# A hybrid decoder layer in float32: eight raw output weight rows requested in one go, diagonal term of the scan turned round, order of matmuls kept into the second half

## The chip, the core and the metric

The kernel runs on one core of a Trainium2 chip. The metric is the device time of one execution in microseconds (us), less is better. The core has five engines with instruction queues of their own: PE (TensorE, matrix products; its weight loads are listed apart as PEld), DVE (VectorE), ACT (ScalarE), POOL (GpSimd) and SP (SyncE, which here only issues DMA transfers). An engine works through its own queue in order; a semaphore holds an instruction until what it needs from another engine or from a transfer is there.

## The reference

One decoder layer for 1024 tokens of width 1024, with 16 meta tokens ahead, so L = 1040 positions, all in float32. The normalized input is projected to z, x, B, C, dt for a state space mixer (SSD, 16 heads of 64, two groups with a state of 128, chunks of 128 positions) and to q, k, v for a stick-breaking attention (16 heads of 64). Both results go through one output matrix, and a feed-forward part (width 2816, with a causal convolution over three positions) follows.

```python
xn = rms_norm(h, mix_pre_g)
proj = xn @ w_in                                  # z, xbc, dt_raw, q, k, v
# SSD, by chunks of 128 positions; the meta tokens are a chunk of 16
dt = softplus(dt_raw + dt_bias); A = -exp(a_log)
Acs = cumsum(dt * A)                              # within a chunk
Ldec = where(causal, exp(Acs[l] - Acs[s]), 0)
CB = einsum('bclgn,bcsgn->bgcls', Cc, Bc)
y_diag = einsum('bgcls,bgjcls,bcsgjp->bclgjp', CB, Ldec, Xdt)
states = einsum('bclgn,bgjcl,bclgjp->bcgjpn', Bc, exp(Acs[-1] - Acs), Xdt)
prev   = scan over chunks: carry * exp(Acs[-1]) + states
y_off = einsum('bclgn,bcgjpn,bgjcl->bclgjp', Cc, prev, exp(Acs))
y = (y_diag + y_off + xs * d_skip) * silu(z);  y_ssd = rms_norm(y, norm_g)
# stick-breaking attention
w[t,s] = beta[t,s] * prod over s<j<t of (1 - beta[t,j]),  beta = sigmoid(q.k / 8)
y_sb = rms_norm(w @ v, sb_norm_g)
mix = concat([y_ssd, y_sb]) @ w_out
h = h + rms_norm(mix, mix_post_g)
xn = rms_norm(h, ffn_pre_g);  gu = xn @ w_up
f = (gelu(causal_dwconv3(gu[:DFF])) * gu[DFF:]) @ w_down
h = h + rms_norm(f, ffn_post_g)
```

## The kernel before

**Precision.** A float32 operand of a projection is kept as two parts of a faster type, a rounded high part and the rest as a low part. A product then is three matmuls: high by high, high by low, low by high. `load_w` (L145) requests a raw weight block of 128 columns into a buffer `wraw` (two of them), ACT copies it into `whi` and POOL subtracts to get `wlo` (three buffers each). `project_steps` (L155) is a generator that yields after each of three stretches of positions (348, 346, 346 columns), eight blocks of the contraction by three matmuls each. `run(steps, n)` advances a generator by n yields, and `flow` strings several together. The source thereby interleaves work by hand: while one stage works through its chunks, `run(fill, ...)` puts projections for the next stage between them.

**Who sets the order.** Over most of the kernel a scheduler orders each engine's instructions by its own estimate. `tc.manual_schedule` (the ExitStacks `pe_order` and `order`) keeps the order of the source instead: for the PE during attention (`pe_order`, opened ahead of the loop over head pairs, closed at the end of it), and for PE, DVE, ACT and POOL from the sixth tile of the second output product on (`order`, opened at `t == 6`).

**Input (0 to 40 us).** For each of nine token blocks the input is normalized and transposed in two halves of four blocks (L215 to L222) into a PSUM tile of the pool `tp` (two tiles); ACT copies the high part `xh` from it, DVE subtracts the low part `xl`.

**First projections (40 to 190 us).** dt (16 columns), B and C of group 0 run side by side (`head`). dt is transposed to positions (`tpd`), DVE works through a chain of some twenty small instructions (softplus as a series), and `decays()` (L427) makes the cumulated decays with three pairs of small matmuls `pz_ea`, `pz_de`, `pz_cd` and exponentials on ACT. It stands after two steps of the first x projection. `bc[0][1][0]()`, the transposition of B, follows two steps later.

**SSD scans (190 to 460 us).** `scan_steps(g)` walks over nine chunks (one of 16 rows, eight of 128). `chunk_weights` (L450) makes `em`, the decayed and masked C by B of eight heads, `xdt`, the inputs times dt, and `yo`, the skip term. `chunk_outputs` (L486) makes the state, the diagonal term `yd` (eight products, `em` as the weights and 64 columns of `xdt` streamed), which DVE adds to `yo`, and the off-diagonal term `yf`. `chunk_store` (L518) transposes `yo` in four blocks into `tp`, multiplies by the gate `zk` and writes the result to memory (`yd` in DRAM, one tile for each 128 positions).

**Attention (460 to 1023 us).** A loop over eight head pairs `p` and eight query blocks `i`. `block_weights` makes logits `z` on the PE, two sigmoids `kp` and `bt` on ACT, the running product on DVE and the weights `bt` on POOL; `block_turn` transposes these (`tw`) and ACT copies them to `th`; `block_mix` multiplies with v (`av`). Projections of the next pairs fill in through `fill` until `p == 6, i == 5`, where they end. `avc` (L651) is the last product of a pair, for the edges of the blocks.

**Output products.** The output matrix has 16 rows of blocks of 128 x 1024, eight for the SSD half and eight for the attention half. `wout_steps` (L701) prepares one row a step: it requests the raw row into `wraw`, ACT scales it by the norm's gain into `wh` (L717, hence `wohb<-worb` in the second half), DVE makes the rest `wl`, and `halo_mm` (L708) multiplies the raw row with the two positions `y0` ahead of the tokens (`halo_y` loads them, two matmuls a row). The first half's rows (`wora`) are prepared from `p == 6, i == 5` on, two steps a block. `split_y` (L743) requests a tile `yk` of 128 positions from DRAM, ACT copies the high part `yh` (L748), POOL subtracts the low part `yl` (L749). `out_steps` makes two halves of 512 columns a tile, each 24 matmuls `mo` (L759) into one accumulator; `ssd_half` runs them for the eight tiles of the first half and writes them to `mixd`. These steps, `first`, are advanced from `p == 7, i == 2` on; what is left when attention ends runs in `for _ in first:` with one row of the second half between any two.

**Second half (1023 to 1181 us).** When attention has ended its memory is closed (`apool.close()`), and the pools `outp` and `est` are opened in its place. `second` prepares the rows `worb`. Then a loop over `t` from 1 to 8 makes the second output product of each tile, adds `mixd`, normalizes (`after`, with the mean squares `ms_mo`), and `turn_x2` transposes the result (`x2tp`, L918) for the feed-forward part. From 1181 us on the feed-forward part runs; its first product is `g0a` (L1068).

The names that the profile shows for DMA queues are those of the issuing engine (SPq is SP's). `f32` records of the PE come in pairs: one float32 matmul shows as two records.

## Time and profile before

| | before |
|---|---|
| device time, median of 3 runs | 1834.47 us (1833.14 to 1835.4) |
| the profiled execution | 1832.72 us |
| its span in the trace | 1831.0 us |
| mean granted clock of the PE over the span | 0.989 |
| bytes moved by DMA | 173.96 MB, 95 GB/s on average |
| share of PE in the chain that ended last | 47% of the span |

The profile was taken of one execution, whose own time is 1.7 us more than its span. Busy time counts records of an engine; matmuls are pipelined, so a record can begin before the one ahead of it has ended, and the time from start to start is what a matmul costs in a row of equal ones.

Three views are shown below. In the busy times by stage, a row is a window (from and to in us from the span's start), its length, then the busy us and the number of records of PE, PEld, DVE, ACT and POOL, the granted clock, the mean busy share of the DMA engines and GB/s. In the list of waits, a row is the waiting instructions, what released them, the total in us, the number of waits and the longest one. In the timeline, a row is the start in us, the length, the engine, line and operation, out<-in, shapes, how many records are drawn together, and in brackets the idle time before it and what ended it.

The 40 slices of the page tell the same coarsely: the PE is busy for nine tenths or more except in the first two, in the last, and in those that begin at 869.7, 1052.8 and 1144.4 us. The first of these three lies where attention runs without projections, the other two in the second output product.

### The profile page before, as it was taken

The numbers are of one execution on the slowest core, as the hardware profiler recorded it, in microseconds if no ns is written. First come the engines' busy times: TensorE is split into PE (matmuls) and PEld (weight loads), VectorE is DVE, ScalarE is ACT, GpSimd is POOL, SyncE is SP. The second block draws the span as 40 slices with busy tenths as digits, with TensorE's granted clock in tenths as the row PEclk, the third lists the DMA queues.
The fourth block names the chain that finished last, engine by engine and source line by source line (L and its number), as shares of the span: only waits on it lengthen the run. The fifth ranks groups of instructions, "written<-read, shape, count | busy, mean of one in ns | idle before, by whom it ended". The sixth has DMA issues, their size and how long they took to land.

```text
span 1831.0 us, 27362 instructions
## 1 busy us (share of the span) xinstructions
PE 1758.9 (96%) x10957; PEld 1508.3 (82%) x10957; DVE 1060.3 (58%) x1142; ACT 829.0 (45%) x1371; POOL 858.5 (47%) x613
## 2 busy tenths in 40 slices
PE   6899999999999999999799989899999999999997
PEld 5899889889888888888478767788889998888886
DVE  5551783574534544544722256766666666667988
ACT  5333454443655655655654243443333333344444
POOL 3213563485644644643764132276777776600001
PEclk9999999999999999999899999999999999999999
DMA  4123242231011110110232455233233333196344
GB/s 155 47 70 119 75 125 96 71 103 54 24 36 36 32 39 28 32 36 11 82 106 70 139 175 181 81 104 92 87 103 111 104 103 99 52 316 230 95 120 160
DMA packets 91443, 173.96 MB, mean 95 GB/s; under 512 B 11722, under 2 KB 36714, under 8 KB 91316
## 3 DMA queue, kind: packets, MB, share of 16 engines
q1 hardware_dynamic: 91316, 172.21, 29.9%
q8 instruction: 86, 1.41, 0.3%
q14 instruction: 41, 0.34, 0.1%
HBM read 122.39 MB, written 49.79 MB: 94 GB/s over the span
## 4 chain that ended last, share of the span: by engine, by line
PE 47%; DVE 3%; ACT 2%; POOL 1%; issue 1%; DMA 1%; POOLq 0%; SPq 0%; ACTq 0%; DVEq 0%
PE dn L1445 11%; PE fX L1054 9%; PE mo L759 6%; PE fY L1054 6%; PE fA L1054 6%; PE tw L617 1%; PE av L631 1%; PE z L596 1%; PE pj_v L163 1%; PE pj_q L163 1%; PE halo L708 1%; PE pj_k L163 1%; DVE oxn L912 1%; DVE mb L903 1%; POOL yl L749 0%
## 5 line engine op out<-in xcount | busy, mean ns | idle before, releaser
L601 DVE TENSOR_TENSOR_SCAN kp<-kp,hold 128x272 f32<-128x272 f32 (+7 forms) x128 | 206.7, 1657 | 202.3 <-ACT kp L597 99.6
L603 POOL TENSOR_TENSOR bt<-bt,kp 128x256 f32<-128x256 f32 (+7 forms) x128 | 213.8, 1688 | 195.9 <-DVE kp L601 143.3
L997 POOL TENSOR_TENSOR wl<-wr,wh 128x1024 fp32r<-128x1024 f32 x44 | 110.7, 2524 | 40.7 <-ACT wh L996 40.7
L1445 PE MATMUL dn<-dl,dh 128*128 128x512 f32 x308 | 120.1, 390 | 0.1
L1445 PE MATMUL dn<-dh 128*128 128x512 f32 x308 | 120.1, 390 | 0.0
L1445 PE MATMUL dn<-dh,dl 128*128 128x512 f32 x308 | 120.0, 390 | 0.0
L1491 POOL TENSOR_TENSOR fms<-fms,nhalf 128x1 f32<-128x1 f32 x8 | 8.5, 1060 | 225.8 <-DMA ar<-fda 186.0
L597 ACT ACTIVATE kp<-z 128x288 f32<-128x288 f32 (+6 forms) x112 | 82.7, 738 | 60.4 <-PE z L596 37.3
L1374 ACT ACTIVATE dh<-ar 128x512 fp32r<-128x512 f32 x77 | 48.7, 632 | 111.2 <-PE dn L1445 88.9
L996 ACT ACTIVATE wh<-wr 128x1024 fp32r<-128x1024 f32 x44 | 46.6, 1060 | 114.9 <-PE fX L1054 68.3
L596 PE MATMUL z<-k,q 64*128 64x144 f32 (+6 forms) x448 | 88.0, 494 | 8.3 <-ACT bt L598 3.9
L1126 DVE SCALAR_TENSOR_TENSOR ga<-gr,pp,ga 128x1024 f32<-128x1024 f32 x44 | 71.4, 1622 | 34.7 <-ACT ga L1119 34.0
L619 ACT ACTIVATE th<-tw 128x1024 f32<-128x1024 f32 (+2 forms) x96 | 74.4, 811 | 33.2 <-PE tw L617 31.1
L598 ACT ACTIVATE bt<-z 128x288 f32<-128x288 f32 (+6 forms) x112 | 83.0, 741 | 0.0
L617 PE MATMUL tw<-ident,bt 128*128 128x128 f32 x576 | 78.3, 282 | 4.4 <-POOL bt L603 2.9
L631 PE MATMUL av<-th,v 128*64 128x128 f32 x1152 | 78.1, 281 | 0.0
L631 PEld LDWEIGHTS av<-th,v 128*64 128x64 f32 x1152 | 62.6, 138 | 18.1 <-issue 17.3
L1375 DVE TENSOR_TENSOR dl<-ar,dh 128x512 fp32r<-128x512 f32 x77 | 53.2, 691 | 41.9 <-ACT dh L1374 41.8
L617 PEld LDWEIGHTS tw<-ident,bt 128*128 128x128 f32 x576 | 62.9, 143 | 15.9 <-issue 10.6
L596 PEld LDWEIGHTS z<-k,q 64*128 64x128 f32 x448 | 37.8, 191 | 39.0 <-issue 15.8
L1445 PEld LDWEIGHTS dn<-dh 128*128 128x128 f32 x308 | 57.8, 188 | 12.3 <-ACT dh L1374 0.3
L1445 PEld LDWEIGHTS dn<-dl,dh 128*128 128x128 f32 x308 | 57.9, 188 | 12.2 <-DVE dl L1375 0.4
(542 smaller groups left out, 5797.1 us busy)
## 6 DMA issues: line engine op xcount, KB each, us to landing
wr<-in_w_up SPq DMA_DIRECT2D x44, 512.0 KB
fds<-ga SPq DMA_DIRECT2D x44, 256.0 KB
b<-in_w_down SPq DMA_DIRECT2D x44, 256.0 KB
ar<-fds SPq DMA_DIRECT2D x44, 256.0 KB
fda<-ga SPq DMA_DIRECT2D x33, 256.0 KB
ar<-fda SPq DMA_DIRECT2D x33, 256.0 KB
yk<-yd SPq DMA_DIRECT2D x16, 512.0 KB
zd<-zt SPq DMA_DIRECT2D x8, 520.0 KB
```

The source lines that it names most:

```text
L596: mm(z[:, j, :w], q[h, t0:t0 + P], k[h, a:a + w], start=True, stop=True)
L597: nc.scalar.activation(kp[:, :, a:a + w], z[:, :, :w], AF.Sigmoid, scale=-QSCALE)
L598: nc.scalar.activation(bt[:, :, a:a + w], z[:, :, :w], AF.Sigmoid, scale=QSCALE)
L601: nc.vector.tensor_tensor_scan(kp[:, j][:, ::-1], kp[:, j][:, ::-1], hold[:, L - n:L][:, ::-1], 0.0, op0=ALU.mult, op1=ALU.max)
L603: nc.gpsimd.tensor_tensor(bt[:, j, 0:m], bt[:, j, 0:m], kp[:, j, 1:m + 1], op=ALU.mult)
L617: nc.tensor.transpose(tw[:, j, b, :], bt[:, j, c0:c0 + P], ident)
L619: nc.scalar.activation(th[:, :, :nb, :], tw[:, :, :nb, :], AF.Copy)
L631: mm(av[halves[j], :], v[:, kb, halves[j]], th[:, j, b, :], start=kb == 0, stop=kb == i)
L759: mm(acc, u[:, k, :], v[:, cs], start=(k == 0 and j == 0), stop=(k == 7 and j == 2))
L997: nc.gpsimd.tensor_tensor(l, raw, h.bitcast(F32), op=ALU.subtract)
L1054: mm(acc[:, c, :nn], u[:, k, :], v[:, k, c0:c0 + nn], start=first and k == 0 and j == 0, stop=k == 3 and j == 2, skip_group_check=not first)
L1445: mm(banks[t], u[:, 0, c], v[:, 1, :], start=(p == 0 and i == 0), stop=(p == NPR - 1 and i == 2))
```

## The change

It has eight parts.

1. The transposes of the input rotate over three PSUM pools (`tp`, `z`, `sd`, six tiles) instead of two tiles of `tp`.
2. dt: the high and the low part of its 16 columns lie side by side in one weight of 32 columns, so each of the eight blocks has two matmuls (with `xh` and `xl`) instead of three. The 32 rows are added up while they are turned to positions: nine products with a matrix `fold` (two identities) take the place of nine transposes.
3. `decays()` stands after four steps of the first x projections and after the transposition of B instead of ahead of them.
4. The diagonal term moves from `chunk_outputs` to `chunk_store`: `xdt` (64 columns) is the weight and `em` (128 columns) is streamed, the result comes transposed and goes into alternating halves of the partitions of `tp`, and the four transposes of `yo` add onto it. The addition on DVE and the accumulator `yd` are gone.
5. First half of the output weights: at `p == 6, i == 4` all eight rows are requested, into `wraw`, `wlo` and `whi` buffers in turn. Four rows are prepared at `i == 5`, the rest at `i == 6`, `halo_store` follows, and the first step of `first` comes at `i == 7` instead of at `p == 7, i == 2`. At `p == 7` one step runs at odd `i` and at `i == 6`. `halo_mm` runs for two rows at a time.
6. Second half: `yh1` (`halo_y`) and all eight rows are requested in one go, into two `wraw` buffers (rows 0, 1, 5, 6) and three new ones `wr` (2, 3, 4, 7). Two rows are prepared between any two steps of `first`, and the second tile is split ahead of the loop over `t`.
7. `pe_order` stays open until `t == 6`, so that the PE keeps the order of the source up to there.
8. A scratch size for dynamic DMAs is given (`dynamic_dma_scratch_size=2048`).

```diff
@@ input
             for hf in range(2):
-                tp = psum_tp(f"xtp{i}_{hf}")
+                tp = (psum_tp, psum_z, psum_sd)[(2 * i + hf) % 3](f"xtp{i}_{hf}")
+                if (2 * i + hf) % 3:
+                    tp = tp.rearrange("p (a b) -> p a b", b=P)
@@ dt
-        head = [project_steps(load_w(w_dt, 16, "dt"), 16, xh, xl, CH, dt_evac, "dt")]
+        fold = sp.tile([32, 16], F32, name="fold", tag="fold")
+        nc.vector.tensor_tensor(fold, ident[:32, 0:16], ident[:32, 16:32], op=ALU.add)
+        def dt_steps():
...
+            nc.scalar.activation(hl[:, :, 0:16], raw, AF.Copy)
+            nc.gpsimd.tensor_tensor(hl[:, :, 16:32], raw, hl[:, :, 0:16].bitcast(F32), op=ALU.subtract)
+            for c0, n in CH:
+                acc = psum_mm(f"pj_dt_{c0}")
+                for k in range(KB):
+                    for j, src in enumerate((xh, xl)):
+                        mm(acc[:32, :n], hl[:, k, :], src[:, k, c0:c0 + n],
+                           start=(k == 0 and j == 0), stop=(k == KB - 1 and j == 1))
+                nc.vector.tensor_copy(dtT[:, c0:c0 + n], acc[:32, :n])
+                yield
+        head = [dt_steps()]
...
-            nc.tensor.transpose(tpd[:nr, i * 16:(i + 1) * 16], dtT[:, c0:c0 + nr], ident[:16, :16])
+            mm(tpd[:nr, i * 16:(i + 1) * 16], dtT[:, c0:c0 + nr], fold, start=True, stop=True)
...
-        run(fill, 2)
+        run(fill, 4)
+        bc[0][1][0]()
         decays()
         tmp.close()
-        run(fill, 2)
-        bc[0][1][0]()
         run(fill)
@@ chunk_outputs
-            yg = psum_sd(f"yd{nm}").rearrange("p (h d) -> p h d", d=64)
-            for h in range(8):
-                mm(yg[:nr, h, :], em[:nr, h, :nr], xdt[:nr, h, :], start=True, stop=True)
-            nc.vector.tensor_tensor(yo[:nr], yg[:nr], yo[:nr], op=ALU.add)
@@ chunk_store
             for b in range(4):
-                nc.tensor.transpose(tp[:, b, :nr], yo2[:nr, b * P:(b + 1) * P], ident[:nr, :nr])
+                for j in range(2):
+                    mm(tp[halves[j], b, :nr], xdt[:nr, 2 * b + j, :], em[:nr, 2 * b + j, :nr],
+                       start=b == 0, stop=False, skip_group_check=True)
+            for b in range(4):
+                mm(tp[:, b, :nr], yo2[:nr, b * P:(b + 1) * P], ident[:nr, :nr], start=False, stop=True,
+                   is_transpose=True, skip_group_check=True)
@@ output weights
+    def raw_w(half, k, tile_):
+        wr = tile_ if tile_ is not None else wp.tile([P, D], F32, tag="wraw", name=f"wor{half}{k}")
+        r0 = (8 * half + k) * P
+        nc.sync.dma_start(out=wr, in_=w_out[r0:r0 + P, :])
+        return wr
...
-            wr = wp.tile([P, D], F32, tag="wraw", name=f"wor{nm}{k}")
-            r0 = (8 * half + k) * P
-            nc.sync.dma_start(out=wr, in_=w_out[r0:r0 + P, :])
+            wr = raws_.pop(0) if raws_ else raw_w(half, k, None)
...
             if len(todo) > 1:
-                halo_mm(*todo.pop(0))
+                for arg in todo:
+                    halo_mm(*arg)
+                todo.clear()
             yield
-        halo_mm(*todo.pop(0))
@@ attention loop
-            run(first, int(p == 7 and i > 4))
+            if p == 6 and i == 4:
+                ahead = [raw_w(0, k, None if k % 3 == 0 and k < 6 else wp_f32(("wlo", "whi", "wlo")[k % 3], f"wora{k}"))
+                         for k in range(8)]
...
-            if p == 7 and i == 1:
+            if p == 6 and i == 6:
                 run(wsteps)
                 halo_store(w1pool, 0, halo)
+                ys1 = [split_y(wp, 0, 1, ("whi", "wlo", WB))]
                 first = ssd_half(wres, ys1)
-            elif p > 5:
-                run(wsteps, 2)
-            if p == 7 and i == 0:
-                ys1 = [split_y(wp, 0, 1, ("whi", "wlo", WB))]
-            run(first, int(p == 7 and i > 1))
+            elif p == 6 and i == 5:
+                run(wsteps, 4)
+            run(first, int(p == 7 and (i % 2 or i > 5) or p == 6 and i == 7))
@@ after attention
     run(meta_steps)
-    pe_order.close()
     apool.close()
...
-    second = wout_steps(op, 1, sb_g, wres2, halo_y(op, 1, sb_g), halo)
+    y0b = halo_y(op, 1, sb_g)
+    ahead = [raw_w(1, k, None if k % 5 < 2 else est.tile([P, D], F32, tag="wr", name=f"worb{k}", bufs=3)) for k in range(8)]
+    second = wout_steps(op, 1, sb_g, wres2, y0b, halo, ahead)
     run(second, 1)
     ys = [split_y(op, 1, 1, ("yh", "yl", 2))]
     for _ in first:
-        run(second, 1)
+        run(second, 2)
     run(second)
+    ys.append(split_y(op, 1, 2, ("yh", "yl", 2)))
@@ second output product
         if t == 6:
+            pe_order.close()
             order.enter_context(tc.manual_schedule(engines=ORDERED))
-        if t < NT - 1:
+        if 1 < t < NT - 1:
             ys.append(split_y(op, 1, t + 1, ("yh", "yl", 2)))
@@ kernel
-    nc = bacc.Bacc("TRN2", target_bir_lowering=False, num_devices=1)
+    nc = bacc.Bacc("TRN2", target_bir_lowering=False, num_devices=1, dynamic_dma_scratch_size=2048)
```

More of the change, by code (lines that the diff above doesn't have):

```diff
@@ L371, in tile_layer @@
         nc.scalar.activation(expa, alog, AF.Exp)
-        dtT = rp.tile([16, L + 3], F32, name="dtT", tag="rt", bufs=1)
-        def dt_evac(acc, c0, n):
-            nc.vector.tensor_copy(dtT[:, c0:c0 + n], acc[:16, :n])
-        head = [project_steps(load_w(w_dt, 16, "dt"), 16, xh, xl, CH, dt_evac, "dt")]
+        dtT = rp.tile([32, L + 3], F32, name="dtT", tag="rt", bufs=1)
+        fold = sp.tile([32, 16], F32, name="fold", tag="fold")
+        nc.vector.tensor_tensor(fold, ident[:32, 0:16], ident[:32, 16:32], op=ALU.add)
+        def dt_steps():
+            raw = wp.tile([P, KB, 16], F32, tag="wraw", name="wr_dt")
+            hl = wp.tile([P, KB, 32], F32R, tag="whi", name="wh_dt", bufs=WB)
+            nc.sync.dma_start(out=raw, in_=w_dt)
+            nc.scalar.activation(hl[:, :, 0:16], raw, AF.Copy)
[9 more added lines that the diff above has]
+        head = [dt_steps()]
         bc = bc_flow(0)
@@ L516, in chunk_outputs, with chunk_store @@
             return yo, zk, nprev
-        def chunk_store(g, c, yo, zk):
+        def chunk_store(g, c, em, xdt, yo, zk):
             nr = NM if c == 0 else P
@@ L548, in scan_steps @@
                 yield
-                chunk_store(g, c, yo, zk)
+                chunk_store(g, c, cur[0], cur[1], yo, zk)
                 cur = nxt
@@ L699, in attend_meta, with wp_f32, wout_steps @@
         nc.gpsimd.tensor_copy(sq[:, M0:NM], sqm[:, 0, :])
-    def wout_steps(pool, half, gain, res, y0, acc):
+    def raw_w(half, k, tile_):
[3 more added lines that the diff above has]
+        return wr
+    def wp_f32(tag, name):
+        return wp.tile([P, 8, P], F32R, tag=tag, name=name, bufs=WB).bitcast(F32).rearrange("p a b -> p (a b)")
+    def wout_steps(pool, half, gain, res, y0, acc, raws_):
         nm = "ab"[half]
@@ L807, in tile_layer @@
                 halo = psum_mm("halo0")
[L808 to L809 removed]
+                wsteps = wout_steps(w1pool, 0, ssd_g, wres, halo_y(w1pool, 0, ssd_g), halo, ahead)
+            if p == 6 and i == 6:
                 run(wsteps)
                 halo_store(w1pool, 0, halo)
+                ys1 = [split_y(wp, 0, 1, ("whi", "wlo", WB))]
                 first = ssd_half(wres, ys1)
[L813 to L817 removed]
+            elif p == 6 and i == 5:
+                run(wsteps, 4)
+            run(first, int(p == 7 and (i % 2 or i > 5) or p == 6 and i == 7))
             if p == 7 and 2 < i < 6:
@@ L858, in tile_layer @@
     for _ in first:
-        run(second, 1)
+        run(second, 2)
     run(second)
-    def wp_f32(tag, name):
-        return wp.tile([P, 8, P], F32R, tag=tag, name=name, bufs=WB).bitcast(F32).rearrange("p a b -> p (a b)")
+    ys.append(split_y(op, 1, 2, ("yh", "yl", 2)))
     yraw[0] = wp_raw
```

1 line of the change is left out of this document (removed).

## The prediction

> **What bounds the kernel now.** I read the head of the page first, then the busy times of the engines by stage, then the list of what the PE waited for.
>
> ```profile
> span 1831.0 us, 27362 instructions
> PE 1758.9 (96%) x10957; PEld 1508.3 (82%) x10957; DVE 1060.3 (58%) x1142; ACT 829.0 (45%) x1371; POOL 858.5 (47%) x613
> ```
>
> ```profile
> 0.00:40.00 40.00, 22.35 (x121) 18.25 (x122) 23.86 (x42) 22.87 (x40) 14.23 (x24) 1.00 0.53 176
> 40.00:190.00 150.00, 143.57 (x897) 136.38 (x895) 61.51 (x71) 48.77 (x93) 34.95 (x22) 0.98 0.25 75
> 190.00:345.00 155.00, 151.33 (x956) 139.81 (x956) 97.53 (x109) 71.99 (x136) 77.95 (x63) 1.00 0.33 100
> 345.00:460.00 115.00, 112.29 (x683) 97.98 (x682) 73.72 (x98) 55.60 (x130) 78.66 (x81) 0.97 0.25 72
> 460.00:862.00 402.00, 400.54 (x3051) 338.19 (x3051) 184.71 (x141) 228.60 (x379) 216.29 (x169) 1.00 0.10 29
> 862.00:1023.00 161.00, 147.00 (x950) 106.52 (x949) 65.00 (x50) 85.62 (x136) 82.88 (x55) 0.97 0.28 86
> 1023.00:1181.00 158.00, 143.11 (x693) 112.78 (x692) 92.82 (x111) 64.84 (x105) 43.55 (x31) 0.97 0.49 157
> 1181.00:1831.00 650.00, 638.66 (x3618) 558.38 (x3616) 461.17 (x524) 250.67 (x357) 310.01 (x169) 1.00 0.39 125
> ```
>
> The stages are: the normalized input; the first projections; the SSD scans of the two head groups (190 to 345, 345 to 460); attention filled with projections; attention without them; the second output product; the feed-forward part. The first number after the length is the PE. It is busy in all but 72 us. In the SSD stages (3.7 and 2.7 us idle) a matmul less is time less; in the stages of 862 to 1181 (14.0 and 14.9 us idle) the order and the loads decide; behind 1181 the change touches nothing.
>
> ```profile
> PE xtp L219 <- DVE ms_pre L188: 10.3, 1, 10.3
> PE xtp L219 <- DVE xl L222: 6.0, 4, 2.2
> PE pz_ea L431 <- DVE s L419: 4.9, 1, 4.9
> PE g0a L1068 <- ACT gr L1074: 4.5, 1, 4.5
> PE x2tp L918 <- DVE ms_mo L188: 3.9, 1, 3.9
> PE yf L511 <- DVE pv L504: 2.9, 2, 2.0
> PE x2tp L918 <- DVE oxn L912: 1.7, 1, 1.7
> ```
>
> **The change part by part.** *Diagonal term of the SSD.* Before, eight products per chunk (two records each) load 128 columns of weights to stream 64. They become the same products turned round, 64 columns of weights and 128 streamed into alternating halves of the output. Attention has exactly this form in av, so the price is on the trace:
>
> ```profile
> 269.06 1.89 PE L507 MATMUL yd<-xdt,em 128*128 128x64 f32 x16
> 270.79 1.08 PE L511 MATMUL yf<-pv,ct 128*128 128x512 f32 x2
> ...
> 713.15 1.75 PE L631 MATMUL av<-th,v 128*64 128x128 f32 x28
> 714.83 1.97 PE L617 MATMUL tw<-ident,bt 128*128 128x128 f32 x16
> ```
>
> From start to start yd takes 1.73 us for 16 records, 108 ns each; av takes 1.68 us for 28, 60 ns each. A chunk saves 16 x 48 ns = 0.77 us, and 16 full chunks save 12.3 us (the two 16-row chunks are not counted). The PE is the bound there, so I count all of it. The 18 additions that leave DVE, and the accumulator that they read, I price at nothing: other work hid them, and the yf wait of 2.9 us, which they may ease, stays outside the sum. Bounds: 0, if DVE takes over as the bound, and 12.3 + 2.9 = 15.2 with the waits for yf gone too.
>
> The turned products are followed by full-width transposes, so the array's tiling changes twice in each chunk. [...] The trace has that very change from av to tw at 714.83, and tw starts before the 1.75 us of the last av are over. [...]
>
> *dt projection.* High and low weights share one 32-column load, so each k has two products instead of three: 24 fewer.
>
> ```profile
> 43.77 0.32 PE L163 MATMUL pj_dt<-xh,wh_dt 128*16 128x346 f32 x1
> ...
> 47.35 0.32 PE L163 MATMUL pj_dt<-xh,wl_dt 128*16 128x346 f32 x1
> ```
>
> These are the first and the last of 24 matmuls, (47.35 - 43.77) / 23 = 156 ns apart, so 24 x 0.156 = 3.7 us go. The copies of 32 rows, the nine small products with the folding matrix in place of nine transposes, and the one addition that builds that matrix cost nothing that I can see; all lie beside other projections.
>
> *Six accumulators for the first transposes instead of two.* The four waits for xl, 6.0 us, are the upper bound, 0 the lower. DVE limits the gain: behind the first wait of 10.3 us, 29.7 us of the first 40 are left, and DVE's 23.86 us lie nearly all in them, so under 6 us can close. The changed order also puts seven tiles' transposes ahead of the first dt product. I take a third of the waits, 2.1 us.
>
> *The decays moved back two projection steps and one transposition.*
>
> ```profile
> 64.19 2.70 DVE L313 TENSOR_SCALAR bt<-craw_B,pp 128x1040 f32<-128x1040 f32 x1 [4.64 <-ACT craw_B L310]
> 85.27 0.31 DVE L419 SCALAR_TENSOR_TENSOR s<-dt,expa 128x144 f32<-128x144 f32 x1
> 85.63 0.23 PE L431 MATMUL pz_ea<-s,tri 16*16 16x16 f32 x2 [4.89 <-DVE s L419]
> 87.85 0.49 PE L163 MATMUL pj_X<-xh,wh_X 128*128 128x348 f32 x1
> 88.72 0.49 PE L163 MATMUL pj_X<-xh,wh_X 128*128 128x348 f32 x1
> ```
>
> The DVE chain starts with the conv of the last B block (64.19) and is ready 21 us later; its order on DVE stays. In the changed order the decays stand 17 projection matmuls (2.7 us) later plus five transposes that came afterwards, but the scheduler keeps only that distance. The 4.9 us wait shrinks by 2.4 to about 2.5 us. Bounds: 0 (the chain slides as well) and 4.9 plus the slow matmuls behind it, (88.72 - 87.85) / 3 = 290 ns against 156, some 20 of them: 2.7 us more. I take 2.4, because 2.5 us of wait remain and the stage of 345 to 460 shows a granted clock of 0.97 with no wait longer than 2.0.
>
> [...]
>
> *First half of the output weights.* Eight raw rows go into eight buffers, two raw and six of the hi and lo buffers, as projections release them; the halo products come as two groups of eight; the first output products start at block 7 of head pair 6 instead of block 2 of pair 7, and are spread thinner.
>
> ```profile
> 878.45 1.03 PE L708 MATMUL halo<-wora,y 128*2 128x512 f32 x4
> 894.60 1.52 PE L596 MATMUL z<-k,q 64*128 64x344 f32 x4 [3.53 <-ACT bt L598]
> 1033.88 1.14 ACT L717 ACTIVATE wohb<-worb,pp 128x1024 fp32r<-128x1024 f32 x1
> ```
>
> A weight row gives the PE 1.03 us, so four rows in one block put 4.1 us of cover where the PE stood 3.53 us. But ACT scales each row, 1.14 us, and in the changed order seven rows, the eight halo copies and a yh stand ahead of the last sigmoids of those blocks, for which the PE waits. Bounds: -7.0 (half of the stage's 14.0 us idle), +4.6 (four scalings earlier, all on the path). I take -2.0, nearer to the middle because both act on the same wait.
>
> *Second half and the kept order.* Until the sixth tile the PE now follows the source: product step, two halo rows, product step, and so on. Before, the scheduler mixed them as data came.
>
> ```profile
> 1021.96 0.65 PE L651 MATMUL avc<-thc,vc 128*64 128x256 f32 x4
> 1024.34 2.40 POOL L662 TENSOR_TENSOR sq<-sq,sqb 128x1024 f32<-128x1024 f32 x1 [20.59 <-ACT sqb L661]
> 1026.88 0.32 SPq L747 DMA_DIRECT2D yk<-yd  x1
> 1032.93 1.05 ACT L748 ACTIVATE yh<-yk 128x1024 fp32r<-128x1024 f32 x1
> 1034.11 2.47 POOL L749 TENSOR_TENSOR yl<-yk,yh 128x1024 fp32r<-128x1024 f32 x1 [7.37 <-ACT yh L748]
> ```
>
> ```profile
> 1037.89 4.38 DMA worb<-in_w_out
> 1119.87 5.70 PE mo L759 x24
> ```
>
> Let T be the end of avc (1022.6). Attention's memory is free at 1026.7, and a transfer into it left at once: T + 4.3. In the changed order SP issues there the halo's y, then rows 2, 3, 4, 5, 6, the first yk of the second half, row 7, and only then the yk of tile 7 of the first half. Row 7 reuses the buffer of row 2, so it waits for a halo product on the PE, and tile 7 waits behind it. On the PE: a step to T + 5.7; y lands and is scaled by about T + 8, a wait of 2.3; two halo rows and a step to 15.8; two halo rows to 17.9. Row 7 goes at about 17, yk 0.3 later, landing 4.4 later (21.7), yh to 22.8, yl to 25.3. The PE stands 4.9 us, does one matmul and stands 2.4. New waits: 9.6 us. Of the old 14.9 us, g0a (4.5) and oxn (1.7) lie behind tile 6 and stay; the other 8.7 I let go, since 16 regular steps of 5.7 us give the norms time. Net +0.9. Bounds: -8.7 and, with transfers one behind another, +19.
>
> *Sum.* -12.3 - 3.7 - 2.1 - 2.4 - 2.0 + 0.9 = -21.6 us. The profiled execution took 1832.7 us, 1.7 more than its span and 1.8 less than the median of 1834.5; the sum gives 1811.1 by its own time and 1812.9 by the median. I say **1812 us**.
>
> **The rivals.** *Both transitions are covered.* The first output products fill every gap and the second half's loads come in time: -7.0 and -8.7 instead of -2.0 and +0.9, 14.6 us lower, 1797 us. For it: 28.9 us idle in these stages. Against it: ACT's load ahead of the sigmoids and row 7 ahead of yk.
>
> *DVE takes over in the SSD stages.* Half of the 12.3 us comes back as waits: 1818 us. For it: the yf waits on DVE. Against it: DVE is busy 97.5 of 155 us and loses work.
>
> *The early request brings nothing.* Rows are there, but ACT's scalings delay the sigmoids: +4.6 instead of -2.0, 1819 us. For it: the wait of 3.53 ends on ACT, not on a load. Against it: these scalings were in that stage before.
>
> [...]
>
> *Slower: the loads behind the attention queue up.* If the eight transfers from row 2 to yk land one behind another at x us each, the new waits are 2.3 + (4.7 + 8x + 3.5 - 17.9) = 8x - 7.4 us. The rest of the sum is -22.5, and 8.7 of old waits go, so the change loses from x = 4.8 on; at 5.2 it is 1835.5 + 2 for the slow clock behind such a wait, about 1837 us. For it: a single row took 4.38. Against it: the second half's stage moved 157 GB/s on average, 3.3 us for 512 KB, with pauses in it.
>
> **How the numbers follow.** Forecast 0.55, covered transitions 0.18, DVE 0.09, ACT 0.07, emptied array 0.03, queued loads 0.08. The likeliest case has its own range of 1804 to 1820. From 1798 to 1826 the range holds the forecast, the three cases near 1819 and nearly half of the covered case. Within 0.2% (3.7 us, about what a measurement of this kernel can tell from no change) lies 0.03 of the queued loads' chance, slower 0.05; faster 0.92.
>
> **What would show it right or wrong.** The turned products 60 ns apart; dt with 48 matmuls; the wait before pz_ea at 2.5 us; the SSD stages shorter by 12 us together with no new PE wait on DVE; a PE wait of about 5 us for yh or yl at the seventh tile of the first half, with row 7 just ahead of it on SP; no wait for ms_mo. The forecast is wrong if the turned products stay at 108 ns, if the stage of 1023 to 1181 grows by over 10 us, or if the first stages keep their length.

## The result and the profile after

The changed kernel takes 1812.9 us (median of 4 runs, 1811.4 to 1813.8) against 1834.9 us of before in the same comparison: a ratio of 0.9879, 95% interval 0.9862 to 0.9896. The forecast was 1812 us, between 1798 and 1826. The profiled execution of after took 1813.8 us, with a span of 1812.1.

So the sum came out. To see whether its terms did, the same points of the work are marked in both traces: the first or the last record of a name, from the timeline of the PE, in us from the span's start. The two traces differ by 18.9 us where the medians differ by 22.0, because the profiled execution of before was faster than all runs of before in this comparison and that of after was its slowest.

| point | before | after | gained up to here | forecast |
|---|---|---|---|---|
| dt turned to positions (first tpd) | 66.6 | 61.1 | 5.5 | 5.8 |
| first state product (st) | 189.2 | 182.0 | 7.2 | 8.2 |
| first attention logits (z) | 440.6 | 419.3 | 21.3 | 20.5 |
| last v projection ends | 863.9 | 841.3 | 22.6 | 20.5 |
| attention ends (avc) | 1022.6, 3 product steps left | 985.4, 6 left | | |
| first product of the second half (mo with wohb) | 1045.1 | 1038.6 | 6.5 | |
| first feed-forward product (g0a) | 1155.4 | 1136.6 | 18.8 | 21.6 |
| end of the span | 1831.0 | 1812.1 | 18.9 | 21.6 |

The product g0a begins at 1155.4 us in before, ahead of the 1181 us from which the description of that kernel lets the feed-forward part run. All of the gain lies ahead of 440 us. Between 440 and 864 us nothing was changed, and the 1.3 us gained there are no more than scatter: from the first z to the last product of the v projection the fourteen traces of this case take 421.4 to 423.4 us. Behind 864 us 3.8 us are lost again. That size is uncertain too: in the six traces with all of the change behind 864 us (after, e1, e6, e7, e8, e11) the stretch from the start of that product to g0a takes 292.6 to 296.5 us, against 291.8 in before. The busy times of both kernels between the last v projection and g0a show where; columns as before (window, length, then busy us and records of PE, PEld, DVE, ACT, POOL, granted clock, DMA share, GB/s). First before, in three stretches: the rest of attention, up to the second half's first product, up to g0a.

```profile
863.90:1022.60 158.70, 144.70 (x937) 104.29 (x935) 64.74 (x49) 85.03 (x135) 82.88 (x55) 0.97 0.28 88
1022.60:1045.10 22.50, 20.74 (x104) 15.53 (x103) 8.39 (x8) 8.30 (x10) 4.87 (x2) 1.00 0.46 133
1045.10:1155.40 110.30, 103.40 (x463) 79.43 (x463) 66.17 (x81) 43.51 (x74) 32.35 (x24) 0.97 0.54 175
```

The same three stretches after:

```profile
841.30:985.40 144.10, 126.10 (x864) 91.29 (x862) 70.16 (x49) 81.32 (x130) 81.16 (x53) 0.96 0.19 62
985.40:1038.60 53.20, 43.05 (x195) 30.89 (x195) 12.98 (x15) 21.29 (x28) 12.12 (x6) 0.90 0.54 184
1038.60:1136.60 98.00, 95.92 (x441) 78.70 (x442) 55.78 (x74) 34.40 (x60) 28.96 (x23) 0.98 0.47 157
```

Three more product steps of 5.7 us (24 products, 5.70 us in before), 17.1 us, are left for the second stretch. Moved back, attention's stretch would be 161.2 us against 158.7 (2.5 lost), the second one 36.1 against 22.5 (13.6 lost), and the third gives 12.3 back. The PE is idle for 10.2 us in the second stretch and its clock falls to 0.90. The list of the PE's waits after names the places (waiting instruction, releaser, total in us, how many, the longest):

```profile
PE xtp L221 <- DVE xn L213: 6.3, 4, 4.3
PE mo L783 <- ACT yh L772: 6.8, 1, 6.8
PE z L612 <- ACT bt L614: 6.0, 3, 4.7
PE tt_B L331 <- DVE bn L327: 2.9, 1, 2.9
PE yt L540 <- DVE yo L526: 2.8, 4, 1.2
PE mo L783 <- POOL yl L773: 2.5, 2, 1.7
PE x2tp L942 <- DVE ms_mo L188: 1.3, 1, 1.3
PE pz_ea L447 <- DVE s L435: 1.0, 1, 1.0
```

The waits of xtp for xl (6.0 us) have become waits for xn (6.3). Gone are those of yf (2.9) and most of that for pz_ea (4.9 became 1.0) and of that for ms_mo (3.9 became 1.3). New are those of mo for yh (6.8), of z for bt (6.0 instead of 3.9), of tt_B for a copy on DVE (2.9) and of the transposes of the output (yt) for their addition (2.8).

One gain stands in no list of waits. `halo_mm` now runs for two rows at a time, and two rows take the PE no longer than one. Two rows before, then four rows after:

```profile
887.11 1.89 PE L708 MATMUL halo<-wora,y 128*2 128x512 f32 x8
```

```profile
863.93 1.90 PE L733 MATMUL halo<-wora,y 128*2 128x512 f32 x16
```

The halo products of all 16 rows keep the PE busy for 14.2 us in before and for 8.0 us in after. Of the 14.2 us 5.1 lay in the third stretch, where five rows were still to be prepared; after has none there. Every run below keeps the rows in pairs, so these 6.3 us are read from the traces and not tested by a run.

The turned products themselves, and the transposes that follow in the other width, from the timeline after:

```profile
260.79 1.09 PE L537 MATMUL yt<-em,xdt 128*64 128x128 f32 x16
261.82 0.44 PE L540 MATMUL yt<-ident,yo 128*128 128x128 f32 x2
```

16 records take 1.03 us, 64 ns each instead of 108. The transposes start 0.06 us before the last product's record ends, so no time shows between the two widths.

The wait at the seventh tile of the first half, from the timelines after of SP, ACT and PE (one fence for each engine):

```profile
1000.04 0.33 SPq L720 DMA_DIRECT2D worb<-in_w_out  x1
1000.42 0.42 SPq L771 DMA_DIRECT2D yk<-yd  x1
```

```profile
1005.75 1.06 ACT L772 ACTIVATE yh<-yk 128x1024 fp32r<-128x1024 f32 x1 [0.59 <-DMA yk<-yd]
```

```profile
1006.86 0.80 PE L783 MATMUL mo<-woha,yh 128*128 128x512 f32 x1 [6.84 <-ACT yh L772]
1009.33 0.79 PE L783 MATMUL mo<-woha,yl 128*128 128x512 f32 x1 [1.68 <-POOL yl L773]
1011.20 0.63 PE L783 MATMUL mo<-wola,yh 128*128 128x512 f32 x1
1011.63 0.63 PE L783 MATMUL mo<-woha,yh 128*128 128x512 f32 x1
```

Row 7 of the weights leaves at 1000.04, when the halo products of rows 2 and 3 have ended, and yk of tile 7 right behind it. The tile lands 5.3 us later, ACT copies its high part, and the PE has stood for 6.8 us; it does one matmul and stands again for the low part. Then its records are 430 ns apart instead of 230: the last row begins at 1011.63, 0.43 us behind the one above it.

### The profile page after: what moved, and what is told of

It is laid out like the page before. It is cut to its first block, busy times and chain, and to the rows that moved or that the text cites. A ratio compares the mean times of both kernels' runs of the same rounds, so it can differ in the third digit from the quotient of the medians.

```text
span 1812.1 us, 27307 instructions
## 1 busy us (share of the span) xinstructions
PE 1738.3 (96%) x10942; PEld 1492.6 (82%) x10942; DVE 1062.2 (59%) x1125; ACT 831.7 (46%) x1373; POOL 863.4 (48%) x613
## 5 line engine op out<-in xcount | busy, mean ns | idle before, releaser
L647 PEld LDWEIGHTS av<-th,v 128*64 128x64 f32 x1152 | 62.8, 138 | 18.9 <-issue 17.9
L1400 DVE TENSOR_TENSOR dl<-ar,dh 128x512 fp32r<-128x512 f32 x77 | 53.2, 691 | 41.9 <-ACT dh L1399 41.9
```

What stands on the lines that cost most here:

```text
L647: mm(av[halves[j], :], v[:, kb, halves[j]], th[:, j, b, :], start=kb == 0, stop=kb == i)
```

## The experiments

Every time is the median of four runs unless it says otherwise, with the ratio to the kernel before of the same comparison.

### Each part of the first 440 us undone by itself

**e1: the diagonal term as before.**

```diff
+            yg = psum_sd(f"yd{nm}").rearrange("p (h d) -> p h d", d=64)
+            for h in range(8):
+                mm(yg[:nr, h, :], em[:nr, h, :nr], xdt[:nr, h, :], start=True, stop=True)
+            nc.vector.tensor_tensor(yo[:nr], yg[:nr], yo[:nr], op=ALU.add)
...
-                for j in range(2):
-                    mm(tp[halves[j], b, :nr], xdt[:nr, 2 * b + j, :], em[:nr, 2 * b + j, :nr], ...)
...
+                nc.tensor.transpose(tp[:, b, :nr], yo2[:nr, b * P:(b + 1) * P], ident[:nr, :nr])
```

> The changed kernel with the diagonal term as before (em as weights, 64 columns streamed, addition on DVE). Theory, the records of the turned products are 60 instead of 108 ns apart and the PE is the bound in the scans: 12.3 us slower than the changed kernel, up to 15.2 with the yf waits back, so about 1826 us, all of it between 182 and 439 us of the span, and the four yt<-yo waits (2.8 us) go. Rival, DVE had taken over as the bound there: only about 6 us slower. [...]

1832.6 us (10 runs), 0.9975 [0.9965, 0.9984]: 19.7 us slower than the changed kernel by the medians, 17.6 by the two ratios. From the first st to the first z the traces show 255.1 us against 237.3, 17.8 more. Two rows of busy times of e1, and two of after, for the two scans:

```profile
181.10:338.00 156.90, 154.02 (x952) 141.74 (x951) 96.55 (x108) 71.67 (x135) 77.07 (x63) 0.98 0.33 99
338.00:436.20 98.20, 95.50 (x575) 83.33 (x571) 70.16 (x87) 47.42 (x114) 65.23 (x59) 0.97 0.25 75
```

```profile
182.00:328.60 146.60, 145.26 (x952) 130.95 (x952) 96.72 (x99) 71.74 (x135) 78.63 (x63) 1.00 0.35 106
328.60:419.30 90.70, 86.99 (x574) 73.01 (x571) 70.02 (x77) 47.99 (x113) 68.53 (x60) 1.00 0.27 79
```

The idle time of the PE is 5.6 us in e1 and 5.1 in after: the yf waits of 2.9 us are exchanged for the yt waits of 2.8. So the difference is in the records, 16 x (1.73 - 1.03) = 11.2 us by their spacing, and in the clock, about 0.02 x 157 + 0.03 x 98 = 6 us. That DVE takes over as the bound is refuted, and the 0.06 us above show no loss between the two widths that would eat the gain. The clock's share was in no expectation, and part of it belongs to e1 alone: from the first st to the first z before takes 251.4 us, and so does e11 below, which has the diagonal term as before too. Against the 237.3 us of after that is 14.1 us for the term; the other 3.7 of e1's 17.8 us come with its lower clock (0.97 over this stretch, 0.99 in before and in e11).

**e6, e7, e8** (one profiled execution each; read at points of the trace, which is finer than the whole time). In e6 the dt projection has 72 matmuls and nine transposes again, in e7 the input transposes have two accumulators, in e8 the decays stand after two steps. In e6 and e7 the edit is part 2 and part 1 of the change in reverse; that of e8 is

```diff
-        run(fill, 4)
-        bc[0][1][0]()
+        run(fill, 2)
         decays()
         tmp.close()
+        run(fill, 2)
+        bc[0][1][0]()
```

> The changed kernel with the dt projection of 72 matmuls and nine transposes. Theory, 24 matmuls of 156 ns: the start of pj_X comes 3.7 us later less the 1.4 us that the nine products with fold took longer than nine transposes (2.1 against 0.7 us), so 2.3 us later. Rival, the wait for the DVE chain takes up what is saved: pz_cd ends at the same time, 88.6 us, within 1 us.

> The changed kernel with two accumulators for the first transposes. Theory as forecast: the last B block of the head ends 2.1 us later (61.2 becomes 63.3), with waits of xtp on xl of about 6 us. Rival, the six accumulators only move the waits from xl to xn and the transposes ahead of the first dt product: within 1 us.

> The changed kernel with the decays after two steps of the first x projection. Theory: the wait before pz_ea is about 5 us again, the wait of 2.9 us before tt_B goes, and the first state product st begins 1 to 2.5 us later than at 182.0. Rival, the chain of DVE slides and both orders wait alike: st begins within 0.5 us of 182.0.

The first st comes 2.5 us later in e6, 2.0 in e7 and 1.1 in e8; that is 5.6 of the 7.2 us gained at st, and no run shows what makes the rest. In e6 the first pj_X comes 1.9 us later and pz_cd ends 2.9 later; it is the matmuls less the dearer turning, not the DVE chain. The rows of tpd after and before show the dearer turning:

```profile
61.12 2.09 PE L406 MATMUL tpd<-fold,dtT 32*16 32x16 f32 x18
```

```profile
66.57 0.68 PE L390 MATMUL tpd<-ident,dtT 16*16 16x16 f32 x9
```

Nine products with fold are 18 records and take 2.1 us, nine transposes took 0.7. In e7 tpd begins at 63.1 instead of 61.1, as forecast, but not for the reason forecast: its waits of xtp are 16.8 us in sum (10.6 and 6.2) and those of after 16.9 (10.6 and 6.3). What after does not have is a wait of 1.7 us of the first dt product for its weights, which POOL is still making; in after more transposes stand ahead of that product. In e8 the wait ahead of pz_ea is 4.4 us, that ahead of tt_B is gone, and tt_X waits 1.1 us, which it does not in after: the move of the decays took 4.5 us of wait away and put 2.9 back. Why tt_B waits, from DVE's timeline after:

```profile
81.58 2.66 DVE L318 SCALAR_TENSOR_TENSOR xsT<-craw_X,pp,xsT 128x1040 f32<-128x1040 f32 x2
84.16 0.27 DVE L327 COPY bn<-tt_B 16x128 f32<-16x128 f32 x1
```

The transposes of B now come ahead of the decays and need a PSUM tile that DVE has to copy; that copy stands behind the chain for dt and the convolution of x.

### The transition into the second half

**e2: the kept order ended where it was before, at the end of attention.**

```diff
     run(meta_steps)
+    pe_order.close()
     apool.close()
...
         if t == 6:
-            pe_order.close()
             order.enter_context(tc.manual_schedule(engines=ORDERED))
```

> The changed kernel with the PE's kept order ended at the end of attention, where it was before. Theory, as forecast: the kept order lets go of the ms_mo and oxn waits in the second half (3.9 and 1.7 us before), and its price is that the PE can't take other work while it waits for tile 7; so without it one of these waits comes back and the tile 7 wait shrinks, within 3 us of the changed kernel in sum. Rival, the kept order brings the gain of the second half: 5 us or more slower. Rival, the kept order is what costs the 8.5 us at tile 7: 5 us or more faster.

1811.5 us, 0.9868 [0.9854, 0.9883]: not told apart from the changed kernel. In its profile the wait for yh is 4.2 us instead of 6.8, since the halo products came ahead, one of them waits 1.8 us for its row, and g0a begins 4.2 us earlier. The wait for ms_mo does not come back; it is 1.0 us. The one for oxn is 1.7 us instead of 0.3, but it is 1.5 to 1.8 us in e1, e6, e7 and e8 as well, which keep the order. So the kept order neither brings the gain of the second half nor makes its loss.

**e3: row 7 requested behind tile 7.**

```diff
-    ahead = [... for k in range(8)]
+    ahead = [... for k in range(7)]
...
-    for _ in first:
+    for n, _ in enumerate(first):
+        if n == 0:
+            ahead.append(raw_w(1, 7, est.tile([P, D], F32, tag="wr", name="worb7", bufs=3)))
         run(second, 2)
```

> The changed kernel with the request for row 7 of the second half behind that of yk for tile 7; nothing else moves. Theory, yk stood on SP behind row 7, which waits for a halo product on the PE: yk is issued about 995 instead of 1000.4 us, the wait for yh falls from 6.8 to 2 or 3 us, the slow clock behind it (mo records 430 ns apart instead of 230) shrinks, 5 to 8 us faster, about 1806 us. Rival, the transfers share the DMA engines (394 GB/s from 992 to 999 us) and yk is late for that: the wait stays above 5 us and the time within 2 us.

1811.5 us, 0.9868 [0.9852, 0.9885]. The expected 5 to 8 us did not come. Its timelines of SP, ACT and PE:

```profile
994.04 0.93 SPq L771 DMA_DIRECT2D yk<-yd  x2
...
1002.09 1.06 ACT L772 ACTIVATE yh<-yk 128x1024 fp32r<-128x1024 f32 x1 [0.29 <-DMA yk<-yd]
...
1003.20 0.49 PE L783 MATMUL mo<-woha,yh 128*128 128x512 f32 x1 [3.34 <-ACT yh L772]
1006.75 0.79 PE L783 MATMUL mo<-woha,yl 128*128 128x512 f32 x1 [3.05 <-POOL yl L773]
```

The tile is requested at 994.5, 6 us earlier, and yet lands only at 1002: 7.5 us for 512 KB, with six requests of the same size just ahead of it. The wait behind SP's queue was real, but behind it stood the transfers themselves. Both readings hold a part; 6.4 us of waits are left of 8.5, and the clock falls as before (mo records 0.42 us apart behind the second one).

**e4: tile 7 requested ahead of the rows.**

```diff
-            if t < NT:
+            if t < NT and t != 6:
                 ys.append(split_y(wp, 0, t + 1, ("whi", "wlo", WB)))
...
     y0b = halo_y(op, 1, sb_g)
+    ys1.append(split_y(wp, 0, 7, ("whi", "wlo", WB)))
```

> The changed kernel with tile 7 of the first half requested ahead of rows 2 to 7, as the first 512 KB after attention. Theory: yh and yl of tile 7 are there before the PE needs them; the waits of 6.8 and 1.7 us and the slow clock behind them (about 2.3 us) go, the rows come one transfer (1.3 us at 394 GB/s) later and may cost that once: 9 to 11 us faster, about 1803 us. Rival, the wait only moves to the rows, since the same bytes must land before the second half begins: under 3 us faster, with halo or mo waits on worb of 5 us or more.

1803.2 us, 0.9825 [0.9809, 0.9840]: 9.8 us faster than the changed kernel by the medians, and 10.9 at g0a. No wait for tile 7 is left, and no wait for one of the rows stands in its list. The order of the requests, and not their number, was the price.

**e12: the second half and its order as before, with the changed first half.**

```diff
+    pe_order.close()
     apool.close()
...
-    ahead = [raw_w(1, k, ...) for k in range(8)]
-    second = wout_steps(op, 1, sb_g, wres2, y0b, halo, ahead)
+    second = wout_steps(op, 1, sb_g, wres2, halo_y(op, 1, sb_g), halo, [])
...
-        run(second, 2)
+        run(second, 1)
...
```

> The changed kernel with the second half's rows requested one by one as before, one row between two product steps, and the scheduler's own order there; the first half stays changed, so six product steps are left when attention ends. Theory: no row stands ahead of tile 7 on SP behind a wait for the PE, and the six steps cover the loads: the wait of 6.8 us is gone, 4 to 9 us faster than the changed kernel, unless the halo's y is late as in e5 (13.3 us). Rival, the request of all rows in one go is what keeps the second half fed: 3 us or more slower.

1801.7 us, 0.9832 [0.9802, 0.9861]: 11.2 us faster than the changed kernel by the medians, 8.6 by the two ratios, which count a run of 1810.9 us among its four. At tile 7 one wait of 2.0 us for yl is left. Its busy times in the three stretches:

```profile
842.00:986.20 144.20, 125.32 (x865) 90.84 (x863) 69.88 (x49) 81.14 (x130) 81.15 (x53) 0.96 0.19 62
986.20:1027.90 41.70, 39.75 (x196) 29.02 (x195) 12.51 (x12) 17.98 (x22) 9.61 (x4) 1.00 0.62 203
1027.90:1124.70 96.80, 94.16 (x443) 77.64 (x443) 61.02 (x77) 37.71 (x67) 33.62 (x24) 1.00 0.52 173
```

The third stretch is 13.5 us shorter than that of before with the same requests and without the kept order. In it the PE is idle for 2.6 us instead of 6.9, the five rows' halo products (5.1 us) are gone, and the clock is 1.00 instead of 0.97, about 3 us. Six product steps are left in the second stretch instead of three, the rows are prepared in their cover, and none is left for the third. The run e5 below shows that this is not the only way to it. The request in one go and the kept order then only cost: the second stretch has 11.5 us more with them (53.2 against 41.7).

**e5: the first half as before, with the changed second half.**

```diff
-            if p == 6 and i == 4:
-                ahead = [raw_w(0, k, ...) for k in range(8)]
+            run(first, int(p == 7 and i > 4))
...
-                wsteps = wout_steps(w1pool, 0, ssd_g, wres, halo_y(w1pool, 0, ssd_g), halo, ahead)
-            if p == 6 and i == 6:
+                wsteps = wout_steps(w1pool, 0, ssd_g, wres, halo_y(w1pool, 0, ssd_g), halo, [])
+            if p == 7 and i == 1:
                 run(wsteps)
...
-            run(first, int(p == 7 and (i % 2 or i > 5) or p == 6 and i == 7))
+            run(first, int(p == 7 and i > 1))
```

> The changed kernel with the first half of the output weights as before (rows requested one by one, two prepared a block, first product step at block 2 of pair 7). Theory: the early request brought about nothing by itself, since the scalings, halo copies and yh on ACT ahead of the sigmoids cost a wait of 4.7 us and a slow clock behind it; time within 4 us of the changed kernel. Rival, as forecast: 2 us or more slower. Rival, the early rows are a loss: 3 us or more faster.

1814.9 us, 0.9894 [0.9877, 0.9910], within 4 us as expected, but not for the reason given. Its busy times in the three stretches, and a new wait in its list, which spoils the run as a measure of the scalings:

```profile
841.60:1001.70 160.10, 144.98 (x936) 104.51 (x934) 66.66 (x49) 85.38 (x135) 83.28 (x55) 0.96 0.26 87
1001.70:1039.90 38.20, 24.90 (x125) 16.75 (x123) 15.76 (x13) 15.52 (x19) 8.05 (x3) 0.82 0.51 167
1039.90:1137.30 97.40, 94.39 (x443) 77.50 (x443) 56.88 (x76) 35.91 (x64) 30.05 (x23) 1.00 0.48 163
```

```profile
PE halo L733 <- DVE y L753: 13.3, 1, 13.3
```

SP requests the halo's y only at 1014.56, after 5.0 us in which it waits for a transfer of mixd to end. The run answers another question, though. Its first half is as before and three product steps are left, and yet its third stretch is as short as that of e12 (97.4 and 96.8 us against 110.3): with two rows between any two steps all eight are prepared ahead of it here too. Either half of the change alone takes the third stretch down by about 13 us, and both together take it down once (12.3).

### What is left, and a version that beats both

**e9: e4, with the scalings of the first half spread and the halo's y loaded early.**

```diff
-            if p == 6 and i == 6:
+            if p == 6 and i == 7:
                 run(wsteps)
                 halo_store(w1pool, 0, halo)
-                ys1 = [split_y(wp, 0, 1, ("whi", "wlo", WB))]
                 first = ssd_half(wres, ys1)
+            elif p == 6 and i == 6:
+                run(wsteps, 2)
+                ys1 = [split_y(wp, 0, 1, ("whi", "wlo", WB))]
...
-            run(first, int(p == 7 and (i % 2 or i > 5) or p == 6 and i == 7))
+            run(first, int(p == 7 and (i % 2 or i > 5 or i == 0)))
...
-    y0b = halo_y(op, 1, sb_g)
+    ys1.append(split_y(wp, 0, 7, ("whi", "wlo", WB)))
+    y0b = halo_y(w1pool, 1, sb_g)
```

> The changed kernel with tile 7 requested first, the halo's y loaded into memory that is free before attention ends, and the first half's scalings spread: four rows at block 5 of pair 6, two at block 6, two and the halo copies at block 7, product steps from block 0 of pair 7 on. Theory: beside the 10 us of e4 the wait of z for bt (4.7 us) with the slow clock behind it (13 us at 0.76, 3 us) goes, and the 1.2 us ahead of the first halo product: 5 to 8 us faster than e4, about 1796 us. Rival, the scalings delay whatever sigmoids they stand among: the waits only move to blocks 6 and 7, within 2 us of e4.

1798.3 us, 0.9801 [0.9783, 0.9820]: 36 us faster than before by the ratio, and 4.8 faster than e4 by the medians (4.4 by the two ratios), a little under the 5 to 8 expected. What it removes is this queue on ACT in the changed kernel, ahead of the sigmoids that the PE waits for:

```profile
865.74 2.23 ACT L740 ACTIVATE woha<-wora,pp 128x1024 fp32r<-128x1024 f32 x2
867.82 1.56 ACT L761 ACTIVATE mh<-halo 2x256 f32<-2x256 f32 x4
869.39 1.06 ACT L772 ACTIVATE yh<-yk 128x1024 fp32r<-128x1024 f32 x1
870.48 0.75 ACT L613 ACTIVATE kp<-z 128x696 f32<-128x696 f32 x1
```

Two scalings, four halo copies and a yh take 4.7 us, as long as z waits. In e9 the longest wait for bt is 2.1 us, and attention's stretch takes 141.1 us instead of 144.2 in e4. Part of the wait moved, part is gone.

**e10: e9 with the edit of e2.**

> The kernel of e9 with the PE's kept order ended at the end of attention. Theory: the kept order cost 2 to 4 us only because the PE could not take the halo products ahead while tile 7 was late; without that stall it is worth nothing either way, within 2 us of e9. Rival, the scheduler's own order is better throughout: 3 us or more faster than e9. Rival, the kept order gains once the stall is gone: 3 us or more slower.

1799.9 us, 0.9811 [0.9792, 0.9830]: within 2 us of e9 as expected, and the two intervals overlap, though all four runs are slower than all four of e9. In the traces e10 has lost 2.4 us on e9 by the first z, far ahead of its edit, and from the end of attention to g0a both take 138.7 us. No worth of the kept order is seen either way.

**e11: only the parts from the output weights on; parts 1 to 4 of the change in reverse.**

> The changed kernel with the input transposes, the dt projection, the decays and the diagonal term as before, so that only the parts from the output weights on are changed. Theory: all the gain lies ahead of 460 us, and what comes behind is a loss of about 3 us by the two profiles: 0 to 5 us slower than before. Rival, as forecast: 1 us faster than before. Rival, the early rows and the kept order carry part of the gain: 5 us or more faster than before.

1836.5 us (10 runs), 1.0015 [1.0002, 1.0028], 2.7 us slower than before by the ratio. That agrees with the 3.8 us lost behind 864 us in the trace of after. Its own trace, of the fastest of its ten runs, loses 0.8 us there.

## Why the prediction was right

The total, the sign and the place of the gain were right, the sizes of several terms were not.

- **Diagonal term, -12.3.** Right in mechanism, close in size: 64 ns instead of 60 make 11.2 us, and with the clock and the waits before and after differ by 14.1 us between st and z, inside the bounds of 0 and 15.2. The additions, which the prediction priced "at nothing", hid an exchange: the yf waits went, as it allowed, and the remaining addition now stands straight ahead of the transposes for 2.8 us.
- **dt, -3.7.** The step that failed is that the nine small products "cost nothing that I can see": they take 1.4 us more than the nine transposes. Measured 2.5 at st.
- **Accumulators, -2.1.** Measured 2.0 in e7, but by luck. The forecast was a third of the waits for xl, and none of the waiting went: it moved from xl to xn (6.0 and 6.3 us). Of the 2.0 us 1.7 are the wait of the first dt product for POOL.
- **Decays, -2.4.** Measured 1.1. The wait ahead of pz_ea fell to 1.0, further than forecast. The step failed because it looked at the moved matmuls alone: the transposes of B, put ahead of them, wait 2.9 us for DVE. That its queue holds their copy behind the chain could be read from "its order on DVE stays".
- **First half, -2.0.** This step failed. By place, attention's stretch lost 2.5 us with the three steps moved back, and is 1.1 us longer than in e5, which has the first half as before. The cover was priced at 4.1 us for four rows; they take 1.90. And the longest wait of z for bt grew from 3.5 to 4.7 us, behind the queue on ACT that the prediction had named; its bound of +4.6 holds the result.
- **Second half with kept order, +0.9.** By place the second stretch lost 13.6 us and the third gave 12.3 back, +1.3, close in sum by other sizes. The new waits at tile 7 were told in place and order, 9.6 us, and measured 9.7 (6.8, 1.7, and 1.2 ahead of the first halo product). Their slow clock, 2.5 us (the 23 records behind the second wait take 8.0 us instead of 5.5), was counted only in the rival of the queued loads. Of the old waits 8.7 us were let go; in the third stretch 4.8 us of idle time went, and with it the five rows' halo products, 5.1 us, which no term holds. The prediction adds up its two terms for the halves. The runs do not: e12 and e5 each get the short third stretch from one half alone, so the second change brings it no second time. Behind the changed first half, the second half as before is 11.2 us faster by the medians.
- **Both halves together.** Their sum, -1.1, was about 4 us too good (2.7 are lost by e11 and 3.8 by the trace of after), although the halo products save 6.3 us that were not counted. That the total still came out at 1812.9 is in part luck: the first 440 us gave 0.8 more than forecast, and the medians happen to lie 3.1 us further apart than the two traces.
- **The rivals.** "Both transitions are covered" was not what the change does; e9 at 1798 us comes close to its 1797, with the requests put in another order. "Queued loads" is not settled by e3: one tile lands after 7.5 us there instead of 4.4, but the x of that rival is the distance from one landing to the next, about 1.3 us for 512 KB at the 394 GB/s from 992 to 999 us. Its sum at x = 5.2 comes to 3.0 us more than before, which is 1837.5 by the median and not 1835.5. For the emptied array of the chances (0.03) the trace of after shows no time: the transposes begin 0.06 us before the last turned product's record ends.

Not settled: how much of the scalings' 4.7 us could be had in a better place, what the pairs of halo rows are worth by themselves, and what the first half would do beside an unchanged second half and unchanged first 440 us. None of these was run.

## What to carry to other kernels

Where several loads are requested in one go, their order can decide (9.8 us between the changed kernel and e4): put first what the engine at the bound needs first, also ahead of loads that it needs in greater number. When two changes each empty the same stage of the same work, their gains do not add up (about 13 us of the third stretch from either here, 12.3 from both): ask of each what is left for it once the other is in. Take the price of an instruction from a row of the same form and grouping as the changed kernel will have (64 ns came instead of the 60 of av, and 1.90 us for four halo rows instead of 4.1). When instructions are moved, follow the copies that free their buffers through the other engine's queue as well (tt_B waits 2.9 us for one here).

## What the runs showed of the hardware

The granted clock falls behind waits of 2 us in some places and not in others. The wait of cb for ct is 2.0 us in before, in e1 and in after; behind it the clock is 0.74 and 0.84 in before (4 us each), 0.50 and 0.74 in e1, and 1.00 in after:

```profile
356.00:360.00 4.00, 3.46 (x26) 3.01 (x24) 3.41 (x5) 1.63 (x6) 0.56 (x1) 0.74 0.00 0
```

```profile
352.00:356.00 4.00, 4.00 (x15) 3.19 (x14) 1.84 (x4) 1.72 (x2) 0.30 (x1) 0.50 0.00 0
```

```profile
340.00:344.00 4.00, 4.00 (x38) 3.56 (x38) 3.76 (x7) 3.19 (x10) 2.38 (x3) 1.00 0.02 4
```

In e1 it also falls to 0.57 from 184 to 188 us with no wait listed ahead, only the short products of the chunk of 16 rows. Why equal waits end differently the runs do not show; in before and in e1 yd waits another 0.54 us for em behind the first wait, while in after no second wait is listed there. After the wait of 6.8 us the records were slow from 1006.9 to 1014.6 (granted clock 0.50), 7.8 us with the second wait of 1.7 among them. A short wait can thus have a price beside its length, and it differs from kernel to kernel: about 6 of the 17.8 us between e1 and after. The other runs of the two bear this out, with a mean clock of 0.982 to 0.986 in the ten of e1 and 0.986 to 0.988 in the four of after.
